# Down projections by seven block products, with tokens on partitions and x kept in DRAM during the FFN

## The chip, the core and the metric

The kernel runs on one core of a Trainium2 chip. The metric is the time of one execution on the device in microseconds. A core has TensorE (PE in the profile), which multiplies a stationary block of 128 x 128 by a moving block of up to 512 columns into PSUM; VectorE (DVE), ScalarE (ACT) and GpSimd (POOL) for work on elements; and SyncE (SP), which issues nearly all DMAs here. Each engine works through its own queue in order and waits on semaphores for the others.

## What is computed

A decoder trunk of two layers over 512 tokens and 1024 channels: layer 0 mixes by a gated short convolution and dilated attention, layer 1 by a Conformer convolution and stick-breaking attention. Each layer ends with the gated MLP that the change is about; everything is float32.

```python
for layer in range(DEPTH):                       # 2; D_MODEL 1024, D_FF 2816, SEQ 512
    h = rms_norm(x, norm_g[layer, 0])
    mix = even_mixer(h, ...) if layer % 2 == 0 else odd_mixer(h, ...)
    x = x + rms_norm(mix, norm_g[layer, 1])
    h = rms_norm(x, norm_g[layer, 2])
    x = x + rms_norm(conv_ffn(h, ...), norm_g[layer, 3])

def conv_ffn(h, w_up, w_conv, b_conv, w_down):
    g, u = jnp.split(h @ w_up, 2, axis=-1)
    g = causal_dwconv(g, w_conv) + b_conv        # 3 taps along the tokens
    return (jax.nn.silu(g) * u) @ w_down
```

## The kernel before

Activations lie with channels on partitions and tokens along the free axis: x is eight tiles of 128 x 512. A float32 product is made of three float32r products: each operand is split into a high part (an ACT cast) and a low part (a DVE subtraction of the high part), and `mm3` issues high x high, high x low and low x high into one PSUM bank. Weights come from DRAM in blocks of 512 KB into `wr` (four buffers) and are split into `wh` and `wl` (six buffers each) by `wsplit`. `Plan` records all instructions and sets their order by itself: a list scheduler with its own costs gives every instruction a due time (`nc.t`, moved by TensorE's work; weights are due `LEAD` = 15.46 us earlier), and each engine takes the ready instruction with the earliest due time.

The FFN (`ffn`) has 22 tiles of 128 hidden channels in three rounds of 8, 7 and 7 (`ROUNDS`). Per tile, two products of 24 matmuls each (gate `pg`, up `pu`) go through `ffn_tile`: DVE scales the gate (`gs`), ACT, DVE and POOL make the convolution, the silu and the scaling (`c`), DVE multiplies (`f`) and ACT and DVE split the result into `act`. At the end of a round the down projection runs with output channels on partitions: per block m of 128 channels, the weights of the round are stationary and `act` is moving, three matmuls per tile into the bank `pp`, which is copied to `y` in the first round and added to it by DVE in the others. In the last round (`last_proj`, `halves`) blocks 6 and 7 are computed in two halves of 256 tokens, so that the post-norm of the first half can start early: squares on ACT, sums over channels by matmuls with a column of ones (`st`), `rsq` on DVE and POOL, broadcast by matmul (`bc`), and `half_x`, which scales y, adds it to x and makes the next layer's `u`. After layer 1, `update` sends x to DRAM as the output.

Beside the FFN of layer 0 run 28 side pieces (`Side`, `Ahead`): weights of the odd mixer are loaded, split and written to DRAM in two parts, so that layer 1 needs no splitting for them; they are due every `SIDE_DT` us. The pool `t4` (`NB_T4` buffers of 4 KB per partition) holds `u`, `act`, `y` and the mixers' tiles; x has its own 16 KB.

Of the kernel before, what the change touches and what calls it, by code (L numbers as in the profile page):

```python
# [27 lines left out]
ROUNDS = ((0, 8), (8, 7), (15, 7))  # L28
# [5 lines left out]
NB_T4 = 25  # L34
# [21 lines left out]
C_T0 = [0.49, -25.54, 38.09, -3.42]  # L56
# [5 lines left out]
LAG_X = 2.62  # L62
LAG_S = 1.22
# [4 lines left out]
SIDE_T0 = 10.0  # L68
SIDE_DT = 12.3
# [127 lines left out]
class Plan:  # L197
# [3 lines left out]
    def __init__(self, nc):  # L201
        self.nc, self.tasks, self.pools, self.t, self.cur = nc, [], {}, 0.0, None
        self.rate, self.floor, self.main, self.depth, self.load = 1.0, None, [], 0, None
# [38 lines left out]
    def in_turn(self, task):  # L242

        task.turn = self.load
        self.load = task
# [168 lines left out]
def trunk_kernel(ctx, tc, xT, vecs, relb, onehot, lnc, maskb,  # L414
                 wf, w1e, wve, woe, w1o, wvo, woo, wup, wd0, wd1, wd2, outT):
    nc = Plan(tc.nc)
    wdn = (wd0, wd1, wd2)
# [11 lines left out]
    def nm(s):  # L429
        cnt[0] += 1  # L430
        return f"{s}{cnt[0]}"
# [39 lines left out]
    x_all = C((P, KD, S), F32, "x")  # L471
    x_t = [x_all[:, k] for k in range(KD)]
# [6 lines left out]
    def wsplit(raw, wh, wl, sl):  # L479
        nc.scalar.copy(wh[:, sl], raw[:, sl])  # L480
        nc.vector.tensor_tensor(wl[:, sl], raw[:, sl], wh[:, sl].bitcast(F32), op=ALU.subtract)

    def walloc(n):
        raw = nc.tile(wpool, (P, n), F32, nm("wr"), "wr", NB_WR)
        wh = nc.tile(wpool, (P, n), F32R, nm("wh"), "wh", NB_WH)
        wl = nc.tile(wpool, (P, n), F32R, nm("wl"), "wl", NB_WH)
        return raw, wh, wl

    def wchunk(src, n):
        if isinstance(src, Ahead):  # L490
            with nc.at(nc.t - LEAD_S):
                wh, wl = (nc.tile(wpool, (P, n), F32R, nm(t), t, NB_WH) for t in ("wh", "wl"))
# [4 lines left out]
        with nc.at(nc.t - LEAD):  # L497
            raw, wh, wl = walloc(n)
            nc.in_turn(nc.sync.dma_start(raw, src))
            wsplit(raw, wh, wl, slice(0, n))  # L500
# [42 lines left out]
    def mm3(ps, ah, al, bh, bl, first, last):  # L543
        with nc.together():
            nc.tensor.matmul(ps, ah, bh, start=first, stop=False)
            nc.tensor.matmul(ps, ah, bl, start=False, stop=False)
            nc.tensor.matmul(ps, al, bh, start=False, stop=last)
# [104 lines left out]
    def half_x(l, i_post, ys, bc, c0, c1, nr, nxt, scaled):  # L652
        for k in range(KD):
# [6 lines left out]
            e = nc.vector if nxt or k in FIN_V else nc.gpsimd  # L660
            e.tensor_tensor(x[:, c0:c1], x[:, c0:c1], y[:, c0:c1], op=ALU.add)
            if nxt:
                make_u(nr, nxt[0], nxt[1], k, c0, c1)
            elif k % FIN_K == FIN_K - 1:
                ks = slice(k + 1 - FIN_K, k + 1)
                nc.sync.dma_start(outT[ks].rearrange("k p s -> p k s")[:, :, c0:c1], x_all[:, ks, c0:c1])
# [554 lines left out]
```

## Time and profile before

| | us |
|---|---|
| median of 3 runs | 1179.97 |
| lowest, highest run | 1177.67, 1180.09 |
| the profiled execution | 1178.16 |
| its span in the profile | 1176.4 |
| PE, DVE, ACT, POOL busy | 1153.2, 735.7, 552.7, 189.5 |
| mean granted clock | 0.992 of full speed |

The page lists busy time by engine, slices of the span, and the costliest groups of instructions. All operations are recorded through one helper line (L372), so groups are told apart by the names of tiles. In a timeline, the difference of two starts is what an instruction costs in a full queue; durations overlap. `x24` means 24 instructions merged into a row; `[idle ... <- ...]` is the engine's idle time before it and what ended it.

### The profile page before, as it was taken

To read this page: it belongs to the slowest core of one execution; us is meant where nothing else is said; L and a number is where in the kernel's file an instruction comes from. 1 tells how busy PE (TensorE), PEld (TensorE's weight loads), DVE (VectorE), ACT (ScalarE), POOL (GpSimd) and SP (SyncE) were. 2 spreads that over 40 slices of the span, in tenths; PEclk is the share of its full clock that TensorE was granted. 3 is DMA by queue.
4 is the path that set the end of the run, shared out by engine and by line. 5 is a ranking of instruction groups with operands and counts; after the bars stand their busy time and mean duration, and the time that the engine had idled before them with its cause. 6 is when DMAs were issued, how large, how long until landed. Compare 5 with 4: busy or idle time off the path is not lost. (4 is left out here: it accounts for less than half of the span.)

```text
span 1176.4 us, 15396 instructions
## 1 busy us (share of the span) xinstructions
PE 1153.2 (98%) x5710; PEld 964.9 (82%) x5710; DVE 735.7 (63%) x1249; ACT 552.7 (47%) x919; POOL 189.5 (16%) x172
## 2 busy tenths in 40 slices
PE   9999999999999999999999999999999999999996
PEld 6788888988888888888898677789888888888885
DVE  7787773687525654665678998749853345445444
ACT  7465443564334433444347677566533234223332
POOL 1400010021000100010016684000310011000103
PEclk9999999999999999999999999999999999999998
DMA  8822322236676667766934624251423232332302
GB/s 280 282 78 88 108 72 90 73 108 197 211 235 199 211 214 236 225 204 226 393 118 178 233 72 145 107 211 41 143 95 103 90 103 79 106 108 86 93 1 72
DMA packets 52794, 173.86 MB, mean 148 GB/s; under 512 B 6440, under 2 KB 8744, under 8 KB 52720
## 3 DMA queue, kind: packets, MB, share of 16 engines
q1 hardware_dynamic: 51232, 167.83, 42.8%
q0 software_dynamic: 1488, 5.06, 1.4%
q8 instruction: 45, 0.74, 0.3%
q14 instruction: 29, 0.24, 0.1%
HBM read 137.19 MB, written 34.10 MB: 146 GB/s over the span
## 5 line engine op out<-in xcount | busy, mean ns | idle before, releaser
L372 ACT CAST wh<-wr 128x1024 fp32r<-128x1024 f32 (+3 forms) x201 | 202.1, 1012 | 344.1 <-PE pp L372 114.0
L372 DVE TENSOR_TENSOR wl<-wr,wh 128x1024 fp32r<-128x1024 f32 (+3 forms) x201 | 236.5, 1181 | 116.5 <-ACT wh L372 98.5
L372 PE MATMUL pp<-act,wh 128*128 128x512 f32 (+1 forms) x760 | 220.2, 374 | 0.0
L372 PE MATMUL pg<-u,wh 128*128 128x512 f32 x640 | 197.5, 390 | 0.0
L372 PE MATMUL pu<-u,wh 128*128 128x512 f32 x640 | 197.0, 389 | 0.0
L372 PEld LDWEIGHTS pp<-act,wh 128*128 128x128 f32 x760 | 139.2, 188 | 25.4
L372 POOL TENSOR_TENSOR c<-c,rbc 128x512 f32<-128x512 f32 x44 | 62.1, 1413 | 531.5 <-ACT c L372 531.5
L372 PE MATMUL pj<-u,wh 128*128 128x512 f32 x448 | 142.6, 400 | 0.0
L372 PE MATMUL pp<-act,wl 128*128 128x512 f32 (+1 forms) x380 | 141.9, 373 | 0.0
L372 PEld LDWEIGHTS pu<-u,wh 128*128 128x128 f32 x640 | 120.1, 188 | 24.9
L372 PEld LDWEIGHTS pg<-u,wh 128*128 128x128 f32 x640 | 119.7, 188 | 24.6
L372 PE MATMUL pg<-u,wl 128*128 128x512 f32 x320 | 124.5, 389 | 0.0
L372 PE MATMUL pu<-u,wl 128*128 128x512 f32 x320 | 124.5, 389 | 0.0
L372 PEld LDWEIGHTS pj<-u,wh 128*128 128x128 f32 x448 | 81.5, 190 | 15.2 <-issue 0.2
L372 PE MATMUL sg<-u,wh 128*128 128x256 f32 (+1 forms) x448 | 91.8, 302 | 0.9 <-ACT wh L372 0.4
L372 PE MATMUL pj<-u,wl 128*128 128x512 f32 x224 | 88.2, 394 | 0.0
L372 DVE TENSOR_TENSOR gs<-pg,rbc 128x512 f32<-128x512 f32 x40 | 27.6, 691 | 87.7 <-PE pg L372 87.6
L372 PEld LDWEIGHTS pp<-act,wl 128*128 128x128 f32 x380 | 71.5, 188 | 12.6
L372 PEld LDWEIGHTS sg<-u,wh 128*128 128x128 f32 x448 | 71.8, 191 | 5.2 <-ACT wh L372 1.6
L372 POOL TENSOR_TENSOR ca<-ca,cp 128x511 f32<-128x511 f32 (+29 forms) x60 | 71.9, 1199 | 16.3 <-ACT cp L372 11.7
L372 DVE TENSOR_TENSOR f<-pu,c 128x512 f32<-128x512 f32 x40 | 27.6, 691 | 74.2 <-POOL c L372 72.8
L372 PEld LDWEIGHTS pg<-u,wl 128*128 128x128 f32 x320 | 60.1, 188 | 12.6
(177 smaller groups left out, 1713.7 us busy)
## 6 DMA issues: line engine op xcount, KB each, us to landing
wr<-in_wup_dram SPq DMA_DIRECT2D x88, 512.0 KB, 3.5
dh<-wh SPq DMA_DIRECT2D x28, 512.0 KB, 3.4
dl<-wl SPq DMA_DIRECT2D x28, 512.0 KB, 5.6
wr<-in_wd_dram SPq DMA_DIRECT2D x32, 448.0 KB, 3.3
wh<-dh SPq DMA_DIRECT2D x28, 512.0 KB, 5.8
wl<-dl SPq DMA_DIRECT2D x28, 512.0 KB, 7.0
wr<-in_w1e_dram SPq DMA_DIRECT2D x16, 512.0 KB, 4.3
wr<-in_w1o_dram SPq DMA_DIRECT2D x16, 512.0 KB, 4.3
```

The source lines that it names most:

```text
L372: i = getattr(e, m)(*[real(x) for x in a], **{n: real(x) for n, x in k.items()})
```

## The change

Tiles are taken in pairs (channels of 2q and 2q+1), tokens in halves of 256 and output channels in halves of 512. The product of a pair is then a 2 x 2 block product, and it is computed by Winograd's form of Strassen's scheme: seven block products in place of eight. `act_parts` makes four sums of activation halves on DVE and splits seven halves of 256 tokens; `down` makes four differences of weight halves on DVE (in place, in the raw weights) and splits seven halves of 512 output channels. The activations are now stationary and the weights moving, so the result has tokens on partitions. Products 1, 6, 7 and 4 accumulate in the banks `dx`, 5 and 3 in `dq`, 2 in `dz` (two banks each, one per 128 tokens); what stands in a bank is added to `yt` between products. There are four rounds of 3, 3, 3 and 2 pairs.

The post-norm is applied per row: ACT squares `yt` with a sum along the free axis, DVE adds the sums, POOL takes the power, ACT and DVE scale the rows, TensorE turns blocks of 128 x 128 back (`ty`), and DVE multiplies by the norm's gain and adds x in one instruction (`turn_x`). x is written to DRAM after the mixer's transition and read again in the last round of the FFN; its 16 KB go to the pool `t4` (29 buffers for 25). The weights' high and low parts are one tile (`wp`) in place of two, casts have a turn of their own, and the side pieces come more densely.

```diff
-ROUNDS = ((0, 8), (8, 7), (15, 7))
+ROUNDS = ((0, 3), (3, 3), (6, 3), (9, 2))
-NB_T4 = 25
+NB_T4 = 29
+LEAD_R = 20.0
-SIDE_T0 = 10.0
-SIDE_DT = 12.3
+SIDE_T0 = 9.416
+SIDE_DT = 7.98
...
+    def turn_x(l, i_post, ys, sums, c0, c1, nr, nxt):
+        ts = range(c0 // P, c1 // P)
+        col = SM("pcol")
+        for t in ts:
+            tsl, c = slice(t, t + 1), SM("c0")
+            nc.vector.scalar_tensor_tensor(c[:, tsl], sums[0][:, tsl], EPS, sums[1][:, tsl],
+                                           op0=ALU.add, op1=ALU.add)
+            nc.gpsimd.tensor_tensor(col[:, tsl], c[:, tsl], mhalf[:, tsl], ALU.pow)
+            nc.scalar.activation(ys[t][:, 0], ys[t][:, 0], AF.Copy, scale=col[:, tsl])
+            nc.vector.tensor_scalar(ys[t][:, 1], ys[t][:, 1], col[:, tsl], None, ALU.mult)
+        n = c1 - c0
+        for k in range(0, KD, 2):
+            ps = PB("ty")
+            with nc.together():
+                for i in range(2):
+                    q, c = divmod((k + i) * P, S)
+                    for t in ts:
+                        o = i * n + t * P - c0
+                        nc.tensor.transpose(out=ps[:, o:o + P], in_=ys[t][:, q, c:c + P], identity=ident)
+            for i in range(2):
+                x = x_t[k + i][:, c0:c1]
+                nc.vector.scalar_tensor_tensor(x, ps[:, i * n:(i + 1) * n], ng(l, i_post, k + i), x,
+                                               op0=ALU.mult, op1=ALU.add)
+                if nxt:
+                    make_u(nr, nxt[0], nxt[1], k + i, c0, c1)
+                else:
+                    nc.sync.dma_start(outT[k + i][:, c0:c1], x)
...
+            if i_post == 1:
+                for k in range(KD):
+                    nc.sync.dma_start(xds[k][:, c0:c1], x_t[k][:, c0:c1])
...
+    def act_parts(f0, f1):
+        h = S // 2
+        c, d = T2("sc"), T2("sd")
+        nc.vector.tensor_tensor(c[:, 0:h], f0[:, h:S], f1[:, h:S], op=ALU.add)
+        nc.vector.tensor_tensor(c[:, h:S], c[:, 0:h], f0[:, 0:h], op=ALU.subtract)
+        nc.vector.tensor_tensor(d[:, 0:h], f0[:, 0:h], f0[:, h:S], op=ALU.subtract)
+        nc.vector.tensor_tensor(d[:, h:S], f1[:, 0:h], c[:, h:S], op=ALU.subtract)
+        a, b, e, g = (T4(n="act") for _ in range(4))
+        split(a[:, 0, 0:h], a[:, 1, 0:h], f0[:, 0:h])
+        for t, src in ((b, f1), (e, c), (g, d)):
+            split(t[:, 0], t[:, 1], src)
...
+    def down(l, q0, nq, acts, ys, first, sums):
...
+        plan = {"1": (X, (0, L), None), "5": (Q, (0, L), (0, R)), "6": (X, (0, L), (1, R)),
+                "3": (Q, (1, R), None), "7": (X, (0, R), (1, R)), "2": (Z, (1, L), None),
+                "4": (X, (1, L), None)}
...
+        def product(n, outs):
+            ps, (wi, wc), less = plan[n]
+            ws = []
+            for rs in raws:
+                with nc.at(nc.t - LEAD):
+                    r = rs[wi][:, wc]
+                    if less:
+                        nc.vector.tensor_tensor(r, rs[less[0]][:, less[1]], r, op=ALU.subtract)
+                    elif n == "4":
+                        nc.vector.tensor_tensor(r, r, rs[0][:, L], op=ALU.subtract)
...
+                    nc.in_turn(wsplit(r, w[:, L], w[:, R], slice(0, h)), "split")
+                    ws.append(w)
+            for t in range(2):
+                sl = slice(t * P, (t + 1) * P)
+                for q, w in enumerate(ws):
+                    a = acts[q][n]
+                    mm3(ps[t], a[:, 0, sl], a[:, 1, sl], w[:, L], w[:, R],
+                        q == 0 and n in "152", q == nq - 1, n in "6374")
+                for m, c in outs:
+                    y = ys[2 * m + t][:, c]
+                    if first and (m, t, c) not in begun:
+                        nc.scalar.copy(y, ps[t])
+                    else:
+                        nc.vector.tensor_tensor(y, y, ps[t], op=ALU.add)
+                    begun.add((m, t, c))
+                    if last and n in "3274":
+                        sq = T2("sq")
+                        nc.scalar.activation(sq, y, AF.Square, scale=D ** -0.5,
+                                             accum_out=sums[c][:, 2 * m + t:2 * m + t + 1])
+        prods = [("1", ((0, 0),)), ("5", ((1, 1),)), ("6", ((0, 1),)), ("3", ((0, 1),))]
+        if last:
+            prods += [("2", ((0, 0),)), None, ("7", ((1, 1),)), ("4", ((1, 0),))]
+        else:
+            prods += [("7", ((1, 1),)), ("2", ((0, 0),)), ("4", ((1, 0),)), None]
```

DVE's queue in the second down round of layer 0, before (`wl`: low part of weights, `pp`: the round's product, `y`: the sum):

```order
L372 TENSOR_TENSOR wl_3961<-wr_3845,wh_3940 128x896
L372 TENSOR_TENSOR y_3105<-y_3105,pp_3929 128x512
L372 TENSOR_TENSOR wl_3978<-wr_3910,wh_3972 128x1024
L372 TENSOR_TENSOR y_3105<-y_3105,pp_3966 128x512
L372 TENSOR_TENSOR wl_4011<-wr_3872,wh_4005 128x896
L372 TENSOR_TENSOR wl_4032<-wr_3952,wh_4016 128x896
L372 TENSOR_TENSOR y_3174<-y_3174,pp_4001 128x512
L372 TENSOR_TENSOR wl_4051<-wr_3988,wh_4038 128x1024
```

The same place after (`wp`: high and low part of weights, `wq`, `wr`: raw weights, `dq`, `dx`: products, `yt`: the sum):

```order
L374 TENSOR_TENSOR wp_4608<-wq_4277,wp_4608 128x512
L374 TENSOR_TENSOR yt_3010<-yt_3010,dq_4539 128x512
L374 TENSOR_TENSOR wp_4621<-wr_4567,wp_4621 128x1024
L374 TENSOR_TENSOR yt_3024<-yt_3024,dq_4555 128x512
L374 TENSOR_TENSOR wr_4253<-wr_4253,wr_4239 128x512
L374 TENSOR_TENSOR wq_4267<-wq_4267,wq_4258 128x512
L374 TENSOR_TENSOR wq_4277<-wq_4277,wq_4272 128x512
L374 TENSOR_TENSOR yt_2948<-yt_2948,dx_4506 128x512
L374 TENSOR_TENSOR wp_4659<-wr_4253,wp_4659 128x512
L374 TENSOR_TENSOR wp_4659<-wq_4267,wp_4659 128x512
L374 TENSOR_TENSOR wp_4670<-wq_4277,wp_4670 128x512
L374 TENSOR_TENSOR yt_2955<-yt_2955,dx_4523 128x512
```

Between two additions to the sum there stood one or two splits of 896 or 1024 columns; now there stand splits and differences of 512 columns, and the additions are nearer together.

TensorE's queue at the end of layer 1, before (`st`: sums over channels, `bc`: broadcast of the norm):

```order
L372 MATMUL pp_9966<-act_9777,wh_9831 128x256 x2
L372 MATMUL pp_9966<-act_9777,wl_9839 128x256
L372 MATMUL st_10075<-onesd,acc_9807 128x1
L372 MATMUL st_10075<-onesd,sq_10069 128x1
L372 MATMUL st_10075<-onesd,acc_9807 128x1
L372 MATMUL st_10075<-onesd,sq_10069 128x1
L372 MATMUL bc_10092<-ident,pcol_10022 128x128 x2
```

After (product 7, then product 4 on the same banks `dx`, then the transposes `ty` of the first half):

```order
L374 MATMUL dx_10181<-wp_10185,act_10068 128x512 x3
L374 MATMUL dx_10181<-wp_10185,act_10231 128x512 x3
L374 MATMUL dx_10194<-wp_10185,act_10068 128x512 x3
L374 MATMUL dx_10194<-wp_10185,act_10231 128x512 x3
L374 MATMUL dx_10181<-wp_10211,act_10042 128x512 x3
L374 MATMUL dx_10181<-wp_10211,act_10198 128x512 x3
L374 MATMUL ty_10327<-ident,yt_8259 128x128
L374 MATMUL ty_10327<-ident,yt_8286 128x128
```

The column sums and the broadcast are gone; the transposes of the first half stand before the last six matmuls, and product 4 follows product 7 on the same two banks.

## Rows read from the trace of the kernel before

**Rows 1.** The page: busy time of each engine over the span, and GB/s by slice

```profile
PE 1153.2 (98%) x5710; PEld 964.9 (82%) x5710; DVE 735.7 (63%) x1249; ACT 552.7 (47%) x919; POOL 189.5 (16%) x172
...
GB/s 280 282 78 88 108 72 90 73 108 197 211 235 199 211 214 236 225 204 226 393 118 178 233 72 145 107 211 41 143 95 103 90 103 79 106 108 86 93 1 72
```

**Rows 2.** Who TensorE waited for, us in total, times, longest: 250:590, then 820:1165

```profile
PE sg L372 <- DVE u L372: 0.2, 1, 0.2
PE sg L372 <- ACT u L372: 0.2, 1, 0.2
...
PE st L372 <- ACT sq L372: 1.0, 1, 1.0
```

**Rows 3.** Stretches: us, then busy us (instructions) by engine, clock, DMA share, GB/s

```profile
261.00:583.00 322.00, 322.00 (x1451) 267.88 (x1450) 180.97 (x210) 132.36 (x160) 28.34 (x21) 1.00 0.69 229
837.00:1158.00 321.00, 321.00 (x1445) 266.90 (x1443) 149.47 (x180) 111.38 (x140) 27.09 (x21) 1.00 0.27 86
```

**Rows 4.** Chain of waits in layer 1's FFN: start, us, what

```profile
889.16 43.52 PE pp L372 x192
...
1008.84 38.08 PE pp L372 x168
...
1158.11 0.79 PE st L372 x8
```

**Rows 5.** Groups by form, down projections against wh: count, busy us, mean ns

```profile
L372 PE MATMUL pp<-act,wh 128*128 128x512 f32 x648 | 199.5, 389 | 0.0
L372 PE MATMUL pp<-act,wh 128*128 128x256 f32 x112 | 20.7, 286 | 0.0
```

**Rows 6.** TensorE's timeline: start, us, instructions; in the mixer and at the end

```profile
67.48 0.60 PE L372 MATMUL tp<-ident,L 128*128 128x128 f32 x4
67.83 0.36 PE L372 MATMUL s<-ks,qs 128*128 128x256 f32 x1
...
1151.83 0.40 PE L372 MATMUL pp<-act,wh 128*128 128x256 f32 x2
...
1152.19 0.40 PE L372 MATMUL pp<-act,wh 128*128 128x256 f32 x2
...
1160.27 0.60 PE L372 MATMUL bc<-ident,pcol 128*128 128x128 f32 x4
1160.63 0.48 PE L372 MATMUL pp<-act,wh 128*128 128x256 f32 x2
```

**Rows 7.** DVE's timeline in the up products of layer 0

```profile
286.14 0.69 DVE L372 TENSOR_TENSOR gs<-pg,rbc 128x512 f32<-128x512 f32 x1 [2.75 <-PE pg L372]
286.75 1.22 DVE L372 TENSOR_TENSOR wl<-wr,wh 128x1024 fp32r<-128x1024 f32 x1
287.88 1.53 DVE L372 SCALAR_TENSOR_TENSOR c<-gs,vec,c 128x511 f32<-128x511 f32 x2
289.33 1.22 DVE L372 TENSOR_TENSOR wl<-wr,wh 128x1024 fp32r<-128x1024 f32 x1
```

**Rows 8.** POOL's timeline in the same stretch

```profile
290.22 1.48 POOL L372 TENSOR_TENSOR c<-c,rbc 128x512 f32<-128x512 f32 x1 [9.40 <-ACT c L372]
301.36 1.30 POOL L372 TENSOR_TENSOR c<-c,rbc 128x512 f32<-128x512 f32 x1 [9.66 <-ACT c L372]
```

**Rows 9.** Timelines at the end of the span: TensorE, ACT, POOL, DVE

```profile
1162.76 0.28 PE L372 MATMUL pp<-act,wl 128*128 128x256 f32 x1
...
1163.69 0.42 ACT L372 ACTIVATE sq<-y 128x256 f32<-128x256 f32 x1 [2.16 <-DVE y L372]
...
1165.88 0.82 POOL L372 TENSOR_TENSOR pcol<-c,mhalf 128x2 f32<-128x2 f32 x1 [0.43 <-DVE c L372]
...
1168.01 2.74 DVE L372 TENSOR_TENSOR y<-y,bc 128x256 f32<-128x256 f32 x8 [1.88 <-PE bc L372]
1170.67 2.09 DVE L372 TENSOR_TENSOR x<-x,y 128x256 f32<-128x256 f32 x3
```

More of the change, by code (lines that the diff above doesn't have):

```diff
@@ L62 @@
 LAG_X = 2.62
+LAG_T = 0.0
+LEAD_R = 20.0
 LAG_S = 1.22
@@ L499, in wchunk @@
             nc.in_turn(nc.sync.dma_start(raw, src))
-            wsplit(raw, wh, wl, slice(0, n))
+            nc.in_turn(wsplit(raw, wh, wl, slice(0, n)), "split")
         return wh, wl
@@ L541, in wtile, with mm3 @@
         return kview(wh), kview(wl)
-    def mm3(ps, ah, al, bh, bl, first, last):
+    def mm3(ps, ah, al, bh, bl, first, last, more=False):
         with nc.together():
-            nc.tensor.matmul(ps, ah, bh, start=first, stop=False)
-            nc.tensor.matmul(ps, ah, bl, start=False, stop=False)
-            nc.tensor.matmul(ps, al, bh, start=False, stop=last)
+            for a, b, start, stop in ((ah, bh, first, False), (ah, bl, False, False), (al, bh, False, last)):
+                nc.tensor.matmul(ps, a, b, start=start, stop=stop, skip_group_check=more)
     def kstep(ps, w, k, r, first, last, c0=0, c1=S):
@@ L670, in transition @@
         pss = [PB("sg") for _ in srcs]
-        update(l, i_post, ys, half, HV, nr, nxt)
+        xds = [nc.tile(dram, (P, S), F32, nm("xd")) for _ in range(KD)]
+        update(l, i_post, ys, half, nr, nxt)
         ws = [wtile(s, KD) for s in srcs]
@@ L678, in transition, with update @@
                 nr.rstd([acc], c0 // P, c1 // P)
-        return nr, pss
-    def update(l, i_post, ys, half, parts, nr=None, nxt=None):
+            if i_post == 1:
+                for k in range(KD):
+                    nc.sync.dma_start(xds[k][:, c0:c1], x_t[k][:, c0:c1])
+        if i_post == 1:
+            x_t[:] = xds
+        return nr, pss
+    def update(l, i_post, ys, half, nr=None, nxt=None):
+        if i_post == 3:
+            d, sums = half
+            for c0, c1 in HV:
+                next(d, None)
+                with nc.at(nc.t + LAG_T, 0.0):
+                    turn_x(l, i_post, ys, sums, c0, c1, nr, nxt)
+            return
         half, scaled = half
         col = SM("pcol")
-        for c0, c1 in parts:
+        for c0, c1 in HV:
             bc = post_rstd(col, half(c0, c1), c0, c1)
-            with nc.at(nc.t + (LAG_X if nxt else FIN_X), 0.0):
+            with nc.at(nc.t + LAG_X, 0.0):
                 half_x(l, i_post, ys, bc, c0, c1, nr, nxt, scaled)
@@ L1125, in trunk_kernel @@
         else:
-            update(l, 3, ys, half, zip(FIN[:-1], FIN[1:]))
+            update(l, 3, ys, half)
     with tc.manual_schedule():
```

107 lines of the change are left out of this document (63 added, 44 removed).

## The prediction

> **What bounds the kernel now.** I read the page first: TensorE is busy 98% of the span, VectorE (DVE) 63%, ScalarE (ACT) 47% [rows 1]. A busy share says little of a limit, so next the list of who waited for whom: between 250 and 590 us (the FFN of layer 0 and the transition behind it) TensorE waits 0.4 us in all, between 820 and 1165 us (the FFN of layer 1) 1.0 us [rows 2]. The table by stretches says the same: in 261 to 583 us and in 837 to 1158 us TensorE is busy for the whole stretch at a granted clock of 1.00 (the upper level, 2.4 GHz), while DVE is busy 180.97 of 322 us and 149.47 of 321 us [rows 3]. So both FFNs are bound by the number of TensorE's instructions, and DVE has room, less in layer 0, where the side pieces (splitting weights of the odd mixer for later) run beside it. The chain of waits gives the price: a down projection of 192 matmuls of 128x512 takes 43.52 us, one of 168 takes 38.08 us [rows 4]; that is 0.2267 us each, with no gap. Matmul durations in the timeline (0.39 us) overlap and are no price.
>
> **Part 1, TensorE's count.** Before, the down projections are 972 matmuls of 128x512 (648 against wh, half as many against wl) and 168 of 128x256 (112 and 56) [rows 5]. Three of the halves take 0.36 us from start to start, 0.12 us each [rows 6]. So 972 x 0.2267 + 168 x 0.12 = 240.5 us. After, the order holds 528 with dx, 264 with dq and 132 with dz as output, 924 in all, each again with 512 moving columns: 209.5 us. Gain **31.0 us**, all on the path, if TensorE stays without gaps.
>
> **Part 2, TensorE's additions.** The turning back is 32 transposes of 128x128 per layer, 64 in all. Four of them take 0.35 us from start to start in the mixer [rows 6], 0.0875 us each. The last 16 stand behind the last matmul and belong to the tail, so 48 x 0.0875 = 4.2 us. Gone are the column sums (0.79 us for eight in layer 1 [rows 4]; layer 0 has four per half, so 0.4 us twice) and the broadcasts (four in 0.36 us [rows 6], three times on the path): 0.79 + 0.8 + 1.08 = 2.7 us. Net cost **1.5 us**. TensorE's part: -29.5 us.
>
> **Part 3, DVE.** It gets 360 more instructions, 1251 to 1611 by the order. Prices from start to start in the busy FFN of layer 0 [rows 7]: a 128x1024 split 1.13 us, a 128x512 operation 0.61 us, two shifted multiply-adds 1.45 us. For 128x256 I take 0.34 us: eight in 2.74 us [rows 9]. Per pair of tiles the change adds four sums of 256 and a split of 256 (1.7 us), three splits of 512 for two (0.6 us), four weight differences (2.4 us) and seven half splits for two of 1024 (4.3 - 2.3 = 2.0 us); per layer 48 additions to y for 18. I summed the order over the stretch that is worst, from the scaled gate (gs) of tile 11 of layer 0 to that of tile 12, which has one up product, the whole second down round and one gate product of TensorE: 5.44 + 28.56 + 5.44 = 39.4 us at 0.2267 us. DVE has there 9 splits of 1024 (10.2), 38 operations of 512 (23.2), two multiply-adds (1.45), five of 256 (1.7): **36.5 us**, 93%. The same counts stand from tile 17 to 18. In layer 1, without side pieces, the like stretch has 6, 35, two and three: 30.6 us, 78%. Over the whole of layer 0, from the gs of tile 2 to that of tile 21, DVE has 217 of 512, 62 of 1024, 52 of 256 and 41 multiply-adds, 250 us beside 292 us of TensorE. So no stretch is over 100% and the work hides beside TensorE; what hides it is thin in two stretches of layer 0 and thick elsewhere. ACT's 144 more instructions of about 0.6 us are half DVE's load and hide too.
>
> How much DVE's in-order queue costs at 93% no row of before shows: it was never so full. Bounds: nothing, as at today's 56%; or each of the seven products in two rounds of layer 0 waits for one DVE operation more, 14 x 0.69 = 9.7 us (0.69 us is the 128x512 operation's whole duration [rows 7]). Below nothing it can't go, since TensorE had only 1.4 us of gaps to give [rows 2]. I take **4 us**, nearer to nothing because the trace shows TensorE untouched wherever DVE had any room, and because six weight buffers (twelve half products of 1.36 us each) let DVE run ahead.
>
> POOL's scaling of the gate is one more thing in that stretch. It takes 1.30 us alone and took 1.48 us where a DVE split that began 0.89 us before it still ran [rows 7, 8]: it seems to have waited for DVE. The Trainium skill (SBUF — State Buffer, Who interferes with whom) says that a DVE instruction with two SBUF inputs and a GpSimd instruction that reads SBUF exclude each other, whoever starts first holding the ports for its whole instruction; the trace agrees at this place, with 1.48 us for 1.30 us. By it the stretch would hold one or two scalings more, 37.8 to 39.1 of 39.4 us.
>
> **Part 4, x in DRAM.** 32 stores of 128 KB and 16 loads of 256 KB, 8 MB in all. The stores are queued on SP behind x's update, ahead of weights, and the loads behind the last down weights, ahead of nothing but the output. DMA's share was 0.69 and 0.27 in the two FFNs [rows 3]; side pieces, 1.57 MB each, now come every 7.98 us in place of 12.3 us of planned time, 197 for 128 GB/s, so layer 0's early part goes from 229 GB/s [rows 3] to about 300. I cost it at nothing: the loads have the last down round (19 us) to land.
>
> **Part 5, the tail.** Before: the last matmul starts at 1162.76 us and ends 0.28 us later; the span ends at 1176.4: **13.4 us**, with square, column sum, POOL's power, broadcast, eight scalings (2.74 us) and additions, the last ending at 1172.76 us, 3.6 us before the end [rows 9]. After, with T the end of the last matmul: eight x additions of the first half stand ahead on DVE and end at about T+0.8; addition to y 0.69, square 0.84 (0.42 for half the width [rows 9]), power 0.82 [rows 9], scaling 0.7, and for the small sum and the handing over between engines 0.75, an estimate: T+4.6; four transposes 0.35; eight x additions at 0.34 to 0.39 us: T+8.0; then the same 3.6 us: T+11.6. Gain **1.8 us**, give or take 2. The transition between the layers keeps its cover: behind product 2's last matmul stand 18 matmuls (4.1 us) before the first transpose, for a chain of addition, square, power and scaling of 3.6 us by the prices above. I take it at nothing.
>
> **Sum.** -31.0 + 1.5 + 4 - 1.8 = -27.3 us on the profiled execution of 1178.16 us (span 1176.4): 1150.9. The median of the three runs, 1179.97, lies 1.8 us above that execution and the lowest, 1177.67, 0.5 below; I add 0.6 and say **1151.5 us**.
>
> **Rivals.** (a) *DVE keeps up everywhere*: no 4 us, 1147.5 us. For it: every stretch sums below TensorE's time. (b) *DVE becomes the bound in layer 0's down rounds*: on top of 36.5 us come two of POOL's scalings, for which DVE stands (2.6 us [rows 8]), and 14 additions to y that stand at the head of DVE's queue until their product ends, 0.2 to 0.35 us each (an estimate), 2.8 to 4.9 us. That is 41.9 to 44.0 us for 39.4, 2.5 to 4.6 us a round, three rounds: 1155 to 1161 us. The rule from the Trainium skill's SBUF page points here. (c) *The product waits for its own bank, and the kernel gets slower*: products 1, 6, 7 and 4 use the same two banks (dx), and each must wait until DVE has added what stands there to y. Between two uses lies one other product (4.1 us), but in the last round 7 and 4 follow each other and only 1.36 us lies between. If DVE's queue is late at each product, all 2 x 4 x 7 = 56 wait; at 0.69 us that is 38.6 us and gives 1147.5 + 38.6 = 1186 us. It is slower from a mean wait of 31.3 / 56 = 0.56 us on. Against it: in layer 1 DVE is idle a fifth of the time. The Trainium skill (Perfetto Trace Analysis, Optimizing Tensor Performance) asks that independent groups rotate through banks so that one's evacuation overlaps the next one's matmuls; here four of seven products share a pair, and no row of before shows such a reuse. (d) *Weights come late*: layer 0's denser side pieces and SP's in-order queue, in which a load that waits for a buffer holds up all behind it. At 5 us for each of the first two rounds, on top of the forecast: 1161.5 us. Against it: the page of before moves up to 393 GB/s in a slice [rows 1]. (e) That the change doesn't do what it says is excluded: the counts come from the built program, and outside the FFNs and what ends them the order on every compute engine is the same as before.
>
> **Chances.** Forecast (waits of 2 to 8 us) 0.50; (a) 0.25; (b) 0.12; (d) 0.04; (c) 0.05; something between that ends within 0.2% of 1180 us (about what a measurement of this kernel can tell from no change) 0.02; a gain above (a), from the tail, 0.02. Faster 0.93, same 0.02, slower 0.05. The range goes from (a) with a tail 3 us better, 1144, to a little above (b) and (d), 1163.
>
> **What would show it.** Matmuls with dx, dq, dz 0.2267 us apart; TensorE's waits in 250 to 560 us no more than some 5 us, named DVE wp or DVE yt; DVE busy about 250 us in layer 0's FFN; no TensorE wait on a DMA; the last matmul some 11.6 us before the end. I am wrong if TensorE's gaps recur at each product, if the transposes cost more than 0.1 us each, or if the mixers' times move, which hold the same instructions in the same order.

## The result and the profile after

The changed kernel takes **1148.59 us** (median; 1147.74 to 1150.34) where the kernel before took 1179.1 beside it: the ratio is **0.9744, 95% interval 0.9726 to 0.9762**. The profiled execution took 1149.34 us, with a span of 1147.5 us. Forecast were 1151.5 us and faster.

The lines of the page that answer to [rows 1] (busy us, share of the span, instructions by engine; GB/s in 40 slices):

```profile
PE 1127.0 (98%) x5518; PEld 937.8 (82%) x5518; DVE 910.6 (79%) x1609; ACT 611.0 (53%) x1079; POOL 201.8 (18%) x166
...
GB/s 282 277 94 93 92 74 92 93 190 177 188 351 341 179 329 334 220 258 148 139 98 226 188 125 92 165 147 176 192 1 129 180 23 74 133 125 37 220 1 73
```

TensorE is busy 26.2 us less, DVE 174.9 us more, and TensorE is still at 98%. The chain of waits (start, us, what) shows the price of a product as the prediction used it, 18 matmuls in 4.08 us, 0.2267 us each:

```profile
1059.85 4.08 PE dx L374 x18
1068.01 4.08 PE dx L374 x18
```

The stretches of the two FFNs, which answer to [rows 3], and three shorter ones in layer 0 (us, then busy us and instructions by engine, granted clock, DMA share, GB/s):

```profile
261.00:567.00 306.00, 304.32 (x1334) 249.39 (x1334) 266.90 (x390) 159.05 (x230) 35.41 (x21) 1.00 0.67 238
820.00:1130.00 310.00, 310.00 (x1369) 256.64 (x1368) 242.64 (x371) 135.75 (x210) 43.44 (x23) 1.00 0.28 95
...
295.00:305.00 10.00, 8.83 (x36) 6.31 (x36) 9.96 (x17) 9.04 (x17) 1.63 (x1) 1.00 0.57 199
...
381.44:420.95 39.51, 39.51 (x175) 32.48 (x174) 36.70 (x54) 21.14 (x30) 2.39 (x2) 1.00 0.68 231
476.61:516.07 39.46, 39.01 (x170) 31.27 (x169) 37.00 (x55) 21.05 (x30) 3.07 (x2) 1.00 0.69 237
```

Layer 1 has no gap. Layer 0 has some, and their size is easily read too small. Whom TensorE waited for there (250 to 560 us; us in total, times, longest), and the same for its weight loads (245 to 580 us):

```profile
PE dq L374 <- ACT act L374: 0.8, 1, 0.8
PE dx L374 <- DVE act L374: 0.5, 2, 0.3
PE dz L374 <- DVE wp L374: 0.2, 1, 0.2
PE dq L374 <- DVE act L374: 0.2, 1, 0.2
...
PEld dx L374 <- DVE act L374: 1.3, 2, 0.7
PEld dq L374 <- ACT act L374: 1.2, 1, 1.2
PEld dq L374 <- DVE act L374: 0.9, 2, 0.6
PEld dz L374 <- DVE wp L374: 0.8, 2, 0.7
PEld dx L374 <- DVE yt L374: 0.8, 3, 0.5
```

The matmuls' list adds up to 1.7 us, the loads' to 5.0. A matmul row lasts 0.39 us though the next one can start 0.2267 us later, so the first 0.16 us of each gap don't show as idle. Counting is surer: the stretch 295 to 305 us holds 36 matmuls where a full one holds 46, some 2 us less of work, where busy time shows 1.17 of idle. A count can be off by one; added up from start to start (what lies above 0.2267 us), the gaps of layer 0 are 2.0 us in the first down round, none in the second, 1.2 in the third and 0.3 in the fourth.

Four marks that every kernel has tell where the time went (us, from the starts in TensorE's timeline: first gate product of layer 0, first product `sg` behind its FFN, first gate product of layer 1, end of the span; the expectations call `sg` a score product):

| kernel | ahead of layer 0's FFN | layer 0's FFN | between | layer 1's FFN and end |
|---|---|---|---|---|
| before | 246.8 | 340.1 | 235.7 | 353.8 |
| after | 246.1 | 329.0 | 235.9 | 336.5 |
| eight products (e1) | 245.2 | 340.2 | 235.3 | 350.9 |
| full dose on DVE (e2) | 244.5 | 374.4 | 235.2 | 349.0 |
| half dose (e10) | 245.6 | 355.2 | 235.5 | 342.4 |
| side pieces as before (e3) | 244.5 | 334.4 | 238.2 | 336.5 |
| x in SBUF (e4) | 246.2 | 328.9 | 236.5 | 336.5 |
| tail's order (e5b) | 246.5 | 329.0 | 235.1 | 335.5 |
| no side subtraction (e6) | 245.7 | 327.4 | 235.8 | 336.5 |
| no POOL scaling (e7) | 246.6 | 326.4 | 235.8 | 337.1 |
| banks in a row (e8) | 245.7 | 339.4 | 236.4 | 336.5 |
| e7 and e5b (e9) | 246.4 | 325.5 | 236.6 | 335.7 |
| e7 and e5b (e11) | 244.9 | 326.0 | 236.0 | 335.6 |
| after, once more (e12) | 246.1 | 329.1 | 236.4 | 336.5 |

The stretch ahead of the FFN differs by 2 us with no relation to an edit; the other columns repeat within some 0.5 us (after and e12). From before to after, layer 0's FFN lost 11.1 us and layer 1's with its end 17.3, of which 2.3 are the tail and 15.0 the FFN.

### The profile page after: what moved, and what is told of

Its sections match the earlier page's. It is cut to its first block, busy times and chain, and to the rows that moved or that the text cites. A ratio compares the mean times of both kernels' runs of the same rounds, so it can differ in the third digit from the quotient of the medians.

```text
span 1147.5 us, 15551 instructions
## 1 busy us (share of the span) xinstructions
PE 1127.0 (98%) x5518; PEld 937.8 (82%) x5518; DVE 910.6 (79%) x1609; ACT 611.0 (53%) x1079; POOL 201.8 (18%) x166
## 4 chain that ended last, share of the span: by engine, by line
PE 77%; DVE 16%; ACT 2%; issue 2%; DMA 1%; POOL 1%; SPq 0%; DVEq 0%; POOLq 0%; ACTq 0%
PE pg L374 18%; PE pu L374 16%; PE dx L374 9%; PE pj L374 8%; PE pp L374 8%; PE sg L374 6%; PE dq L374 4%; DVE cv L374 3%; DVE wp L374 3%; PE dz L374 2%; DVE z L374 2%; PE pv L374 2%; PE po L374 1%; DVE L L374 1%; DVE pt L374 1%
## 5 line engine op out<-in xcount | busy, mean ns | idle before, releaser
L374 ACT CAST wp<-wr 128x1024 fp32r<-128x1024 f32 (+2 forms) x209 | 189.5, 914 | 213.7 <-PE pg L374 47.1
L374 DVE TENSOR_TENSOR wp<-wr,wp 128x1024 fp32r<-128x1024 f32 (+2 forms) x209 | 223.8, 1080 | 69.5 <-ACT wp L374 68.9
L374 PE MATMUL pg<-u,wp 128*128 128x512 f32 x960 | 225.6, 390 | 0.0
L374 PE MATMUL pu<-u,wp 128*128 128x512 f32 x960 | 224.1, 389 | 0.0
L374 PEld LDWEIGHTS pu<-u,wp 128*128 128x128 f32 x960 | 180.2, 188 | 37.4
L374 PEld LDWEIGHTS pg<-u,wp 128*128 128x128 f32 x960 | 179.8, 188 | 37.1
L374 PE MATMUL pj<-u,wp 128*128 128x512 f32 x672 | 165.2, 398 | 0.0
L374 PEld LDWEIGHTS pj<-u,wp 128*128 128x128 f32 x672 | 124.0, 190 | 24.6 <-ACT fr L374 0.4
L374 PE MATMUL dx<-wp,act 128*128 128x512 f32 x528 | 127.4, 390 | 0.5 <-DVE act L374 0.5
L374 PEld LDWEIGHTS dx<-wp,act 128*128 128x128 f32 x528 | 98.5, 188 | 22.5 <-DVE act L374 1.3
L374 PEld LDWEIGHTS dq<-wp,act 128*128 128x128 f32 x264 | 49.3, 188 | 12.3 <-ACT act L374 1.2
```

The costliest lines, as they stand in the source:

```text
L374: i = getattr(e, m)(*[real(x) for x in a], **{n: real(x) for n, x in k.items()})
```

## The experiments

The theory: the gain is TensorE's count; layer 0 gives some of it back because work for a product comes late. The rivals: the gain comes from something else that the change brought (tail, spacing, buffers), or the products wait at their banks.

**Eight products.** All of the change but the seven products:

```diff
+                    a = acts[q // 2][q % 2]
...
+                        q == 0, q == 2 * nq - 1)
...
-        prods = [("1", ((0, 0),)), ("5", ((1, 1),)), ("6", ((0, 1),)), ("3", ((0, 1),))]
...
+        prods = [(0, 0, X), (0, 1, Q), (1, 0, Z), (1, 1, X)]
```

> One part undone: each down projection again multiplies all eight block products (1056 matmuls of 128x512 in place of 924), without sums of activation parts and without weight differences; tokens on partitions, the norm per row, the turning back, x in DRAM and the side pieces stay as in the changed kernel. Theory (the gain is TensorE's count, at 0.2267 us a matmul and nothing else): 132 x 0.2267 = 29.9 us more than the changed kernel's 1148.6, less up to 2 us of waits on DVE that go: 1176.5 to 1178.5, about the kernel before. Rival (the gain comes from the tail, the side pieces' spacing or the pools, and the seven products give part of it back in waits): 1150 to 1165.

Measured: 1173.81 us, ratio 0.9966 (0.9954 to 0.9977). Layer 0's FFN takes 340.2 us and layer 1's, to its last matmul, 340.4, as before. So the seven products give 25.2 us by the medians (24.0 by the spans); the rest of the change gives 0.34%, about 4 us, of which 2.9 are the tail. The 1176.5 of the theory was missed by 2.7 us: 3.8 us of waits went, not 2, and the end behind the last matmul is 0.5 us shorter (10.5 for 11.0). In layer 1 the 66 matmuls fewer (15.0 us at 0.2267) gave 340.4 - 325.4 = 15.0 us; in layer 0 340.2 - 329.0 = 11.1. **Layer 0 loses 3.8 us** (3.9 in the expectations, from rounded numbers), and that loss is what the other experiments look for.

**A dose of DVE work**, 128x512 and then 128x256, ahead of each half split of a down weight:

```diff
+                    nc.vector.tensor_tensor(r, r, r, op=ALU.max)
                     if not spare:
                         spare.extend(wpair(D))
```

> A dose of DVE work: the changed kernel with one more DVE operation (r = max(r, r), 128x512, in place, which changes no value) ahead of each half split of a down weight: 77 a layer x 0.61 = 47 us more DVE work in each FFN. Theory (DVE's work is free as long as a stretch holds less of it than of TensorE's): layer 1 goes from 243 to 290 us of 310, free but for single waits (0 to 3 us); layer 0 goes from 267 to 314 us of 306, so it must pass TensorE there by 8 us or more, in the stretches with a down round: 8 to 15 us in all, 1157 to 1164, nearly all of it in layer 0. Rival (each product waits for DVE's queue whatever DVE's share, so every added operation lies on the path in part): 20 to 40 us in both layers alike, 1169 to 1189.

Measured: 1207.58 us (1.0242; 1.0224 to 1.026): 45.4 us more in layer 0, 13.0 in layer 1 (to its last matmul). The theory failed on both, for it had reckoned with the mean over the FFN. The dose all falls into the stretch around a down round, and there the prediction's own sums go over TensorE's 39.4 us: 36.5 + 21 x 0.61 = 49.3 us in layer 0, 43.4 in layer 1, in three rounds and a shorter one 36 and 15 us. The half dose was to tell the two rules apart.

> Half the dose: in front of each half split of a down weight one more DVE operation of half the width (128x256, 0.34 us from start to start; 77 a layer, 26 us; no value changes). It tells apart two rules. Rule 1 (the mean over the FFN decides): layer 0 has 267 + 26 = 293 us of 306, layer 1 243 + 26 = 269 of 310, so nothing is lost: 1148.6 to 1150. Rule 2 (the sum of each stretch with a down round decides): a round of three pairs gets 21 x 0.34 = 7.1 us, layer 0's stretch goes from 36.5 to 43.6 us of TensorE's 39.4, 4.2 us over in each of three rounds and 2 us in the last, some 14 to 17 us and what the granted clock loses in the waits; layer 1's goes from 30.6 to 37.7, below 39.4, 0 to 2 us: 1162 to 1168 in all, nearly all in layer 0. By the same rule the full dose gives 9.9 and 4.0 us a round, 36 and 15 us; measured were 45 and 13.

Measured: 1182.42 us (1.0038; 1.0023 to 1.0053): 0.4% above the kernel before. It takes 26.2 us more in layer 0 and 6.4 in layer 1 (to its last matmul), so the mean is no rule at all, and the sum by stretch is one from below: 14 to 17 and 0 to 2 were expected. What the sum lacks is seen in the half dose's timeline (start, us, engine, what), in layer 0's second down round:

```profile
405.31 0.68 DVE L374 TENSOR_TENSOR wr<-wr,wr 128x512 f32<-128x512 f32 x1
...
405.59 6.09 POOL L374 TENSOR_TENSOR c<-c,rbc 128x512 f32<-128x512 f32 x1 [5.14 <-ACT c L374]
405.92 0.68 DVE L374 TENSOR_TENSOR wq<-wq,wq 128x512 f32<-128x512 f32 x1
406.52 1.21 DVE L374 TENSOR_TENSOR wp<-wr,wp 128x1024 fp32r<-128x1024 f32 x1
...
410.47 1.27 DVE L374 TENSOR_TENSOR yt<-yt,dx 128x512 f32<-128x512 f32 x2
411.19 4.72 PE L374 MATMUL dx<-wp,act 128*128 128x512 f32 x12 [4.55 <-DVE yt L374]
...
412.00 0.68 DVE L374 TENSOR_TENSOR f<-pu,c 128x512 f32<-128x512 f32 x1
```

POOL's scaling of the gate takes 6.09 us where it takes 1.30 alone [rows 8]. From 405.31 to 410.47 us DVE has one instruction behind the other whose operands all lie in SBUF; at 410.47 comes one that reads PSUM, and 411.68 us, when POOL ends, is 1.2 us behind that. So POOL worked when DVE's queue first let it. Behind POOL stand `f`, the sums and the activation parts of the third pair, and the product that takes them. Two more things are in these rows: the product on `dx` waited 4.55 us for DVE to add the bank to `yt`, which is the prediction's rival (c) once DVE is full; and its 12 matmuls take 4.6 us (to the next product's start at 415.75) where 12 took 2.7 us at a granted clock of 1.00. The two stretches' granted clock (the number behind the POOL column):

```profile
405.00:415.00 10.00, 5.00 (x13) 3.71 (x14) 9.95 (x21) 4.41 (x7) 6.09 (x1) 0.66 0.48 157
415.00:425.00 10.00, 9.68 (x41) 7.28 (x41) 10.00 (x17) 5.19 (x9) 0.00 (x0) 1.00 0.71 237
```

The granted clock is 0.66 in the stretch with the wait, between its lower level (0.5, 1.2 GHz) and the upper one, and back at 1.00 in the next. So a wait costs more than its length here, and DVE's overload costs more than its sum.

**POOL's scaling taken out.** The norm of the FFN's input is one factor per token. It is needed in the gate, ahead of the silu; in `f` it can stay out, since it comes through the down projection as a factor of a row of `yt`, and the row is normed. Only the norm's epsilon has to be divided by its square:

```diff
+        if ec is not None:
+            nc.vector.tensor_scalar(ec[:, t0:t1], c0[:, t0:t1], EPS, None, ALU.mult)
...
-            nc.vector.scalar_tensor_tensor(c[:, tsl], sums[0][:, tsl], EPS, sums[1][:, tsl],
+            nc.vector.scalar_tensor_tensor(c[:, tsl], sums[0][:, tsl], ec[:, tsl], sums[1][:, tsl],
...
-        nc.gpsimd.tensor_tensor(c, c, bc, op=ALU.mult)
```

> POOL's scaling of the gate by the input norm (44 times, mean 1.87 us where it took 1.41 before the change) is taken out: the factor is one per token, so it is left in the output of the down projection and cancels in the norm behind it, whose epsilon is divided by its square (one small DVE operation a norm more; what is computed stays the same). DVE's work stays as it is. Theory A (POOL's scaling, which waits for DVE, stands in the chain Silu, scaling, up gate, sums, activation parts, for which the product of the third pair waits): the chain gets 1.6 to 1.9 us shorter, layer 0's loss of 3.9 us falls to 1 to 2: 1146 to 1147. Theory B (the loss is DVE's amount alone): within 0.5 us of 1148.6. Rival C (DVE, which then no longer waits for POOL, does other work ahead of what a product waits for, or the planner's order gets worse): 1150 to 1155.

Measured: 1146.77 us (0.9735; 0.9722 to 0.9749). Layer 0's FFN takes 326.4 us for 329.0 (326.0 and 325.5 in two runs of the same FFN further down, for 325.2 without any loss), with DVE at 267.05 us of busy time for 270.20 in 250 to 560 us. Theory A's times came out. That the scaling's place in the chain is the reason isn't shown by them alone, for `Plan` sets the order anew for each kernel: without the scaling, DVE, ACT and TensorE all run another order around the first down round, where 2.0 of the 3.8 us go. After, this place reads (start, us, engine, what; idle and what ended it):

```profile
286.46 0.62 ACT L374 CAST wp<-wr 128x512 fp32r<-128x512 f32 x1 [4.73 <-DMA dl<-wp]
...
287.12 0.69 DVE L374 TENSOR_TENSOR wp<-wr,wp 128x512 fp32r<-128x512 f32 x1 [1.25 <-ACT wp L374]
...
288.11 1.45 POOL L374 TENSOR_TENSOR c<-c,rbc 128x512 f32<-128x512 f32 x1 [12.27 <-ACT c L374]
288.33 1.78 DVE L374 TENSOR_TENSOR wp<-wq,wp 128x512 fp32r<-128x512 f32 x1
...
295.06 0.63 ACT L374 ACTIVATE c<-c 128x512 f32<-128x512 f32 x1 [2.17 <-DVE c L374]
...
295.77 1.63 POOL L374 TENSOR_TENSOR c<-c,rbc 128x512 f32<-128x512 f32 x1 [6.21 <-ACT c L374]
296.24 2.31 DVE L374 TENSOR_TENSOR wp<-wq,wp 128x512 fp32r<-128x512 f32 x2
...
298.47 0.68 DVE L374 TENSOR_TENSOR f<-pu,c 128x512 f32<-128x512 f32 x1
...
301.11 0.62 ACT L374 CAST act<-sc 128x512 fp32r<-128x512 f32 x1 [0.79 <-DVE sc L374]
...
301.78 0.73 PE L374 MATMUL dq<-wp,act 128*128 128x512 f32 x2 [0.77 <-ACT act L374]
```

and without POOL's scaling:

```profile
289.67 0.63 ACT L374 ACTIVATE c<-c 128x512 f32<-128x512 f32 x1 [0.87 <-DVE c L374]
...
291.24 4.24 PE L374 MATMUL dx<-wp,act 128*128 128x512 f32 x18
...
291.51 0.69 DVE L374 TENSOR_TENSOR f<-pu,c 128x512 f32<-128x512 f32 x1 [0.80 <-PE pu L374]
...
294.70 0.62 ACT L374 CAST act<-sc 128x512 fp32r<-128x512 f32 x1 [0.64 <-DVE sc L374]
...
295.32 4.24 PE L374 MATMUL dq<-wp,act 128*128 128x512 f32 x18
```

The silu of the last tile comes 5.4 us earlier, and 6.4 us earlier the cast `act<-sc` for which product 5 (`dq`) had waited; the products run 18 matmuls in a row. That is more than POOL's own 1.6 us. Three hold-ups stand in DVE's queue ahead of the last tile's `f`. Two come from POOL, and there the hold-up goes the other way: the split of 512 columns at 288.33 and the first of the two at 296.24, which began while POOL's scaling ran, took 1.78 and 1.71 us in place of 0.68, 2.1 us more together. The third doesn't come from the scaling: ACT stood for 4.73 us, up to 286.46, until the store of a side piece's low part (`dl`) had landed and the buffer that it was to write was free, and for 1.25 us DVE waited for ACT. The kernels after, e12, e4, e5b and e8 all have this wait of ACT, 4.6 to 4.8 us long, and lose 2 us or more in the first round; e7, e9, e11, e6 and e3 have no wait for a store there, and lose 0 to 0.6 us.

DVE's amount is not what differs (255 to 305 us, after and without the scaling; busy us of PE, PEld, DVE, ACT, and POOL where it works):

```profile
255.00:305.00 50.00, 48.83 (x213) 39.45 (x212) 47.65 (x74) 29.84 (x50) 12.04 (x6) 1.00 0.54 188
255.00:305.00 50.00, 50.00 (x222) 41.44 (x221) 47.38 (x79) 32.29 (x52) 0.00 (x0) 1.00 0.55 191
```

So POOL's scaling is one link of the chain. What the scaling, the wait for the store and the order each take of the 2.0 us, no run separates.

**DVE's side work taken out** in layer 0, 28 subtractions of 128x1024, with all DMAs left:

```diff
-            wsplit(raw, wh, wl, slice(0, KD * P))
+            nc.scalar.copy(wh, raw)
             nc.sync.dma_start(self.h, wh.bitcast(F32))
-            nc.sync.dma_start(self.l, wl.bitcast(F32))
+            nc.sync.dma_start(self.l, wh.bitcast(F32))
```

> DVE work taken out of layer 0's FFN alone: the 28 side pieces keep their loads, stores and ACT's rounding, but DVE's subtraction (128x1024, 1.1 to 1.2 us each) is left out and the rounded half is stored twice, so the odd mixer's result is not the reference's. Against the run with eight products the changed kernel gains 15.0 us from the first gate product to the last down matmul of layer 1, but only 11.1 us over layer 0's FFN: 3.9 us are lost there. Theory (DVE's amount in layer 0's stretches of 36.5 of 39.4 us causes this loss): with about three side pieces fewer a stretch, 33 us of 39.4, the loss goes: layer 0's FFN takes 325 to 326 us in place of 329.0, 1144.5 to 1146 in all. Rival (the loss comes from POOL's scaling in the chain to the last activation pair, or from the order of the queue, not from its load): 1148 to 1149.

Measured: 1145.19 us (0.9725; 0.9711 to 0.9739), layer 0's FFN 327.4 us. Expected were 325 to 326: 29 us less of DVE work (240.76 us busy for 270.20 in 250 to 560 us) give back 1.6 of the 3.8 us, POOL's 22 scalings out give 2.6 to 3.6. So DVE's amount alone doesn't cause the loss, and the rival alone doesn't fit either. This kernel has another order too: its first round has no gap, and its second has waits of TensorE at 392.84 and 402.34 us (0.38 and 0.61 us of idle time, both ended by ACT), where the changed kernel has none.

**The side pieces' spacing** as before the change (`SIDE_T0` 10.0, `SIDE_DT` 12.3):

> One part undone: the side pieces start and follow each other as in the kernel before (10.0 and 12.3 us of planned time in place of 9.416 and 7.98), so that fewer stand in the early rounds of layer 0 and the rest come in a heap at its end. Theory (layer 0's loss of 3.9 us comes from the chain to the third pair's last activations, in which DVE's side work is one part: without any of it the FFN of layer 0 took 327.4 in place of 329.0 us): the early rounds lose 1 to 2 us less, the heap at the end costs as much: 1147.5 to 1150. Rival (DMA's share sets something in layer 0, and the earlier pieces were needed or were harmful): over 3 us either way.

Measured: 1156.36 us (0.9825; 0.9807 to 0.9842), 7.7 us more, outside the theory; layer 0's FFN 334.4 us and the stretch behind it 238.2. Of the 28 pieces' first stores six now stand behind 545 us, where the changed kernel has none. There the granted clock fell as well:

```profile
555.00:565.00 10.00, 8.15 (x27) 5.65 (x26) 10.00 (x19) 3.80 (x6) 0.00 (x0) 0.83 0.93 309
565.00:575.00 10.00, 8.92 (x39) 6.79 (x37) 9.46 (x16) 6.62 (x14) 0.55 (x1) 1.00 0.96 355
```

66 matmuls for 92 are 5.9 us, lost while DVE is full with the heap. The theory had the first round right (0.6 us of gaps for 2.0, though DVE is about as busy there, 47.44 us of 255 to 305) and the heap's price wrong. The rival's size came true. All of TensorE's waits are put down to DVE and ACT, none to a DMA; but DMA's share is 0.93 and 0.96 in these rows, and ACT waited 0.84 us for a store at 562.70 us, so a part of the DMAs is not excluded.

**The banks in a row.** Products 6, 7 and 4, on the same two banks, directly behind each other:

```diff
-            prods += [("7", ((1, 1),)), ("2", ((0, 0),)), ("4", ((1, 0),)), None]
+            prods = [("1", ((0, 0),)), ("5", ((1, 1),)), ("2", ((0, 0),)), ("6", ((0, 1),)),
+                     ("7", ((1, 1),)), ("4", ((1, 0),)), ("3", ((0, 1),)), None]
```

> Order of the products alone: in all rounds but the last 6, 7 and 4, which add onto the same two banks, follow each other directly (1, 5, 2, 6, 7, 4, 3 in place of 1, 5, 6, 3, 7, 2, 4), so that between two uses of a bank lie 9 matmuls (2.04 us) and no longer 27 (6.1 us). Theory (DVE takes a bank up soon enough wherever it has room): layer 1 free, 0 to 4 us in layer 0: 1148.6 to 1152.6. Rival (c) of the prediction (DVE's queue is late at each product, a reuse waits for it): 6 rounds x 4 waits x 0.69 = 16.6 us or more, in both layers: 1165.

Measured: 1160.05 us (0.9848; 0.9835 to 0.9862). Layer 1 doesn't change (336.5 us), layer 0's FFN takes 10.4 us more. But the two banks in a row aren't it, as TensorE's timeline shows, in layer 0's first and third round and in layer 1's first:

```profile
309.34 0.50 PE L374 MATMUL dq<-wp,act 128*128 128x512 f32 x1 [1.42 <-ACT wp L374]
310.19 1.43 PE L374 MATMUL dq<-wp,act 128*128 128x512 f32 x5 [0.35 <-DVE wp L374]
311.46 8.32 PE L374 MATMUL dx<-wp,act 128*128 128x512 f32 x36
319.62 2.88 PE L374 MATMUL dq<-wp,act 128*128 128x512 f32 x12
...
505.86 0.47 PE L374 MATMUL dq<-wp,act 128*128 128x512 f32 x1 [1.96 <-DVE yt L374]
...
878.35 12.43 PE L374 MATMUL dx<-wp,act 128*128 128x512 f32 x54
890.62 4.24 PE L374 MATMUL dq<-wp,act 128*128 128x512 f32 x18
```

In layer 1 the 54 matmuls of the three products take 12.27 us from start to start, 0.2272 us each; in layer 0 the 36 of products 7 and 4 take 8.16 us, 0.2267 each: no gap between uses of these banks. The waits in layer 0 add up to 8.9 us; most are those of `dq` for weights and of `dx` and `dz` for activation parts, but the longest, 1.96 us at 505.86, is for a bank: product 3 waits until DVE has added product 5 from `dq`. So it speaks against rival (c) for layer 1 and for the pair `dx`, and in layer 0 it shows one wait of that kind. It is no clean test of what the order costs, since the order also moved when weights and parts are needed.

**x in SBUF**, without its stores and loads:

```diff
-        if i_post == 1:
-            x_t[:] = xds
...
-                xd, _ = x_t[:], xtiles()
-                for k in range(KD):
-                    nc.in_turn(nc.sync.dma_start(x_t[k], xd[k]))
```

> One part undone: x stays in SBUF in the FFNs (no stores, no loads), with the same 29 buffers of 128x1024; the order of the compute engines stays as in the changed kernel but for eight DVE rows. Theory (the trip to DRAM is what makes room for a round's twelve activation buffers and four weight buffers; the trip itself costs nothing): three of 32 buffers are missing in each round of three pairs, weights or activations of the third pair wait for the first products' end, 4 to 8 us in each of six rounds: 1170 to 1200. Rival (there is room enough, the trip is only ballast): within 2 us of 1148.6, or a little below.

Measured: 1149.94 us (0.9757; 0.9742 to 0.9771): no difference from the changed kernel, and TensorE's list of waits in layer 0 is the same to the digit. The rival holds; the count of buffers behind the theory was wrong, and where it was wrong stays open.

**The tail's order**, the last six matmuls ahead of the first half's turning back:

```diff
-LAG_T = 0.0
+LAG_T, LAG_F = 0.0, 6.0
...
-                with nc.at(nc.t + LAG_T, 0.0):
+                with nc.at(nc.t + (LAG_T if nxt or c0 else LAG_F), 0.0):
```

> A change of order in the tail alone: behind the last layer's first half the turning back and x's additions are put behind the last six matmuls, and on DVE behind the second half's addition, sum and scaling, so that the longer chain (last matmul, addition to y, square, power, scaling, transposes, additions, output) finds DVE empty. Theory (the tail is that one chain, and eight x additions of 3.2 us stand ahead of its last part): the chain gets shorter by about 1.3 us (transposes that lie ahead of the last six matmuls on TensorE, 1.66 us for 16), 1147.3. Rival (the outputs' stores and the 16 additions in a row behind the last scaling set the end): 0 to 2 us later, since the first half's additions now come last.

Measured: 1147.96 us (0.9739; 0.9724 to 0.9753); from the first gate product of layer 1 to the end 335.5 us for 336.5. By the medians alone it can't be told from the changed kernel; the timeline shows the theory's step at about three quarters of its size.

**Both edits** (the scaling and the tail), twice, the second time beside the changed kernel:

> Two edits together: without POOL's scaling of the gate (the factor cancels in the norm behind), and with the tail's order of the last six matmuls ahead of the first half's turning back. Theory: their gains add, 0.6 to 1.3 us from the tail and 1.5 to 2.5 us from layer 0: 1145 to 1147. Rival (DVE's amount alone sets layer 0's loss): only the tail's part stays, 1147.5 to 1148.

> The kernel of both edits (no POOL scaling of the gate; the last six matmuls ahead of the first half's turning back) beside the changed kernel on one chip. Theory: 2.0 to 3.4 us below the changed kernel (its span was 1144.1 for 1147.5): 0.9973 of before, against 0.9744 for the changed kernel, that is 0.9720 to 0.9732. Rival: no difference, 0.9744.

> The changed kernel itself once more, on the same chip as the other three, so that differences of 2 us can be read: 1148.6, layer 0's FFN 329.0 us from the first gate product to the first score product behind it, layer 1's 325.4 us to the last matmul.

Measured: 1146.26 us (0.9731; 0.9717 to 0.9744), then **1145.68 us (0.9725; 0.971 to 0.9739)** beside **1148.73 us (0.9754; 0.9739 to 0.9768)** for the changed kernel: 3.0 us less by the medians. That is the fastest of the kernels that leave nothing out.

## Why the prediction was right, step by step

**Part 1 (count)** holds: 0.2267 us a matmul with no gap in layer 1, where the eight products cost exactly 66 x 0.2267 = 15.0 us more.

**Part 2 (transposes)** was too low by a little: 16 take 1.66 us (1133.19 to 1134.85 us), 0.104 us each for 0.0875, so 48 are 0.8 us more. That is above the 0.1 us each that the prediction named as a sign of being wrong; the sign came true at this small price.

**Part 3 (DVE)**: the amounts hold. The stretch that was summed to 36.5 us has 36.70 us of busy time in 381.44 to 420.95 us, its twin 37.00; layer 1's like has 31.06 for 30.6 (944.29 to 983.73 us); the 250 us from tile 2 to tile 21 came out at 258.25 (253.44 to 548.71 us), hold-ups included. The 4 us for the queue were measured at 3.8 in layer 0 (329.0 - (340.2 - 15.0)) and nothing in layer 1. That the two figures are so near is luck: 4 was chosen between 0 and 9.7, and its place and reason were not those of that step. The loss isn't spread over products: 2.0 of 3.8 us stand in the first round, whose stretch wasn't summed and where DVE is busy 47.65 us of 50, and the second round's stretch above has no gap at all. The prediction expected waits named DVE wp or DVE yt; TensorE's list names `act`, of ACT and DVE, for 1.5 of 1.7 us. And two links make DVE's load felt there. One is POOL, which the prediction had put into rival (b): its scaling takes 1.869 us in the mean for 1.413 before, and the kernels without it, which run another order too, lose 0.2 to 1.2 us. The other is ACT's wait for the store of a side piece, which the prediction didn't have.

The prediction weighed there what the Trainium skill (SBUF — State Buffer, Who interferes with whom) says, that a DVE instruction with two SBUF inputs and a GpSimd instruction that reads SBUF hold each other up. The rows of the half dose and of the changed kernel agree in both directions, with 6.09 for 1.30 us on POOL and 1.78 for 0.68 on DVE.

**Part 4 (x and side pieces)**: nothing, as costed, for x (e4). For the spacing the prediction looked at the rate of the DMAs alone; what the denser pieces do is to keep the side work out of the last round, and the old spacing costs 7.7 us.

**Part 5 (tail)**: 11.0 us for 11.6. With T = 1136.49 the steps are (timeline of the end):

```profile
1133.99 3.22 DVE L374 SCALAR_TENSOR_TENSOR x<-ty,vec,x 128x256 f32<-128x256 f32 x8
...
1137.13 0.68 DVE L374 TENSOR_TENSOR yt<-yt,dx 128x512 f32<-128x512 f32 x1
...
1139.17 0.54 POOL L374 TENSOR_TENSOR pcol<-c,mhalf 128x1 f32<-128x1 f32 x1 [0.67 <-DVE c L374]
...
1140.29 2.83 PE L374 MATMUL ty<-ident,yt 128*128 128x128 f32 x15 [0.89 <-DVE yt L374]
1140.87 3.23 DVE L374 SCALAR_TENSOR_TENSOR x<-ty,vec,x 128x256 f32<-128x256 f32 x8 [0.64 <-PE ty L374]
```

First half's additions to T + 0.7 (0.8), last addition to T + 7.6 (8.0), and 3.4 us (3.6) to the end; the power takes 0.54 us for the 0.82 that was used.

**The sum**: the span fell by 28.9 us where 27.3 were summed: 0.5 from the tail, 0.7 ahead of the first FFN, where nothing changes, and the rest single tenths. The 0.6 us added for the median went the wrong way; the median of after lies 0.75 us below its profiled execution. Together 2.9 us.

**The rivals.** (a) gave 1147.5, nearer to the time than the forecast's 1151.5, and is still not what happened: DVE did not keep up everywhere. The time alone would have confirmed the wrong case. (b) named one of the links, but its 2.5 to 4.6 us a round came out at 3.8 us for all rounds together. It does become true with 7 us more of DVE work in a round, which takes the kernel 0.4% above the one before. (c) hardly occurs in the change (three waits of weight loads for `yt`, 0.8 us); even 2.04 us between two uses are enough in layer 1 (e8). It occurs when DVE is overfull, with 4.55 us in one wait, and once each in e8 (1.96 us) and in e7, where a wait of 0.64 us for `yt` is the only one left. (d): no TensorE wait is put down to a DMA, and no weights came late for it; but a store of the denser side pieces held ACT for 4.73 us in the first round.

The advice of the Trainium skill (Perfetto Trace Analysis, Optimizing Tensor Performance) that groups rotate through banks was weighed with (c). Here two banks in turn are rotation enough: three products on one pair follow each other at 0.2272 us a matmul (e8, layer 1).

What stays open: how the 3.8 us divide between DVE's amount, POOL's scaling, ACT's wait for a store and the order that `Plan` sets, since each edit moves several of them, and why the order of e8 costs 10.4 us in layer 0 and nothing in layer 1.

## What to carry to other kernels

When a change trades TensorE work for DVE work, sum DVE over the narrowest stretch in which the products need it, not over the phase: here stretches at 93 to 95% lost from nothing to 2 us, and at 111% the loss was more than the whole gain. Then look for links through other engines and through buffers that a store still holds, which such load stretches, and take them out of the chain; a factor per token that a later norm cancels needs no multiplication. Count matmuls per stretch to size a loss, since the list of waits showed 1.7 of 3.8 us here.

## What the runs showed of the hardware

Two things were larger than expected. POOL's multiplication of 128x512, 1.30 us alone, took up to 6.1 us in layer 0 of the half dose behind DVE instructions that follow each other with all operands in SBUF, and it ended 1.2 us after DVE took up one that reads PSUM (three cases: scalings that began at 287.32, 394.88 and 405.59 us and took 6.10, 5.57 and 6.09 us; the DVE instructions began at 292.18, 399.22 and 410.47). The longest, in layer 1 of the full dose, began at 894.44 us and took 9.66; the DVE instruction that reads PSUM began at 902.86.

And TensorE's granted clock lay between its two levels, at 0.63 to 0.84, over stretches of 10 us in layer 0 of the two dosed kernels, whose longest waits were 1.6 to 5.6 us; it was 0.83 to 0.85 after waits of 0.4 and 1.4 us in e3 and of 2.0 and 0.6 us in e8. A wait of 1.4 us by itself (e8, up to 489.43 us) and one of 2.2 us in layer 1 (half dose, up to 894.04 us) left it at 1.00, and the changed kernel, with waits below 1 us, has 1.00 in every such stretch of layer 0.
